# Feed-forward of a decoder block: quadrant sums of the weights made by accumulating transfers instead of VectorE

## The chip, the cores and the metric

One Trainium2 chip, one core. The time is that of the device for one launch, in microseconds (us), as the median of several runs; beside it stands one profiled execution, from which all rows come. TensorE is PE, its weight loads PEld, VectorE is DVE, ScalarE is ACT, GpSimd is POOL, SyncE is SP. Transfers are issued from the queues of SP and of POOL, and 16 DMA engines carry them.

## The reference

One layer for 512 tokens of width 2048, in float32: a sliding-window attention and a gated linear recurrence side by side, merged, projected and added to the input, and then a dense feed-forward. The change touches the feed-forward alone:

```python
x = x + gate1 * rmsnorm(y, g_post_mix[l])
h = rmsnorm(x, g_pre_ffn[l]) * (1.0 + scale2) + shift2
gu = h @ w_ffn_in[l]                       # 2048 x 11264
g_ffn, u_ffn = jnp.split(gu, 2, axis=-1)
y = (jax.nn.silu(g_ffn) * u_ffn) @ w_ffn_out[l]   # 5632 x 2048
x = x + gate2 * rmsnorm(y, g_post_ffn[l])
```

## The kernel before

Every product is made of three matmuls: each operand is split into a rounded part (`hi`, cast by ACT, line 136) and the rest (`lo`, subtracted by DVE, line 137), and TensorE adds hi*hi, hi*lo and lo*hi (lines 908 to 910). A weight chunk is 128 x 1024 float32, 512 KB. It feeds 12 matmuls of 512 columns.

Both matrices of the feed-forward are multiplied by a seven-product scheme for 2 x 2 blocks: weights and activations are cut into four quadrants, and each of the seven products takes a quadrant, or a sum or difference of quadrants, on either side. `weight_form` fetches the weight side of product i for chunk c. Products 1, 2 and 3 take a quadrant as it is; 5, 6, 7 and 4 take combinations, of which 5, 6 and 4 are built up one from the other in a buffer that is kept (`kept["t", c]`).

The up stage (`up_product`) goes through 11 groups of hidden columns, each with 7 products of 4 chunks. Its weights lie in a pool `ffs`, tag `bq`, 10 buffers; the split ones in `ffw`, tags `bhi` and `blo`, 3 buffers each. Two groups run their products 1 and 2 first, while the second half of the tokens is still being normed (`norm1`), turned and put into forms (`to_h2_second`). Products add up in pairs of PSUM banks; ACT copies them out (line 931), and DVE adds later ones (`add`, line 936). What comes out of a group is turned, combined and split into seven forms, which `put` writes to DRAM (`f_dram`, line 987, from POOL's queue, tile `fs`, 2 buffers).

The down stage runs in two parts, of 6 and of 5 groups, each part with 7 products of 12 and 10 chunks. For each pair of chunks a form is read back (`fa`, line 1105, POOL's queue, 6 buffers). Kept weights have a pool of their own (`dlt`, tag `tq`, 12), the others `dlq`, tag `bq`, 15.

PE's order is written out by hand; DVE, ACT, POOL and SP are ordered by a scheduler that follows priorities (`tc.high_priority`). Pools lie on a stack: `ffw` and `ffs` take the place of the pools of the stage before (`stage`, with `wraw`, `whi`, `wlo`; `G1`; `xr`, `G1b`, `junk` of the norm), so a first use waits for the last reader of what lay there.

Of the kernel before, what the change touches and what calls it, by code (L numbers as in the profile page):

```python
# [15 lines left out]
P = 128  # L16
# [57 lines left out]
def kernel(  # L74
# [568 lines left out]
    with tc.tile_pool(name="mrg", bufs=1, reuse_waits="tile") as mp:  # L643
# [13 lines left out]
        def late_ada(pool, i, post):  # L657
# [13 lines left out]
            else:  # L671
# [6 lines left out]
                nc.vector.tensor_tensor(out=dst, in0=dst, in1=pm, op=ALU.mult)  # L678
# [75 lines left out]
    def turn(half, c, neg=False):  # L754
        pt = bg_bank().rearrange("p (k i t) -> p k i t", k=2, i=2)
        for kk in range(2):
            k = 2 * c + kk
            for i in range(2):
                nc.tensor.transpose(pt[:, kk, i], y1[half][:, i, k * P:(k + 1) * P], ident)
        for kk in range(2):  # L760
            k = 2 * c + kk
            t, at = (nab, k - 8) if neg else (ab[:, 1], k)
            nc.scalar.activation(out=rows(half, c)[:, kk], in_=pt[:, kk], func=AF.Identity, scale=t[:, 0, at:at + 1],
                                 bias=t[:, 1, at:at + 1])
# [11 lines left out]
    fx = []  # L776

    def neg_split(hi, lo, src):
        nc.scalar.mul(hi, src, -1.0)
        nc.vector.scalar_tensor_tensor(out=lo, in0=src, scalar=-1.0, in1=hi.bitcast(F32), op0=ALU.mult, op1=ALU.subtract)  # L780

    def to_h2_second(wait):

        yield wait
        fx.extend((ffs.tile([P, 3, 2, 256], F32R, name=f"fxh{c}"), ffs.tile([P, 3, 2, 256], F32R, name=f"fxl{c}"))
                  for c in range(4))
# [4 lines left out]
        for c in range(4):  # L791
            turn(1, c + 4, True)
            split(*places(apair[c + 4], 1), rows(1, c + 4))
            yield 1
            turn(1, c)
            nc.vector.tensor_tensor(out=rows(1, c + 4), in0=rows(1, c), in1=rows(1, c + 4), op=ALU.subtract)
            split(*places(apair[c], 1), rows(1, c + 4))
            yield 1
# [69 lines left out]
    def weight_form(i, c, load, kept, keep):  # L868

        if i == 1:  # L870
            b = load(0, 0, c, "t" if keep else "b")
            if keep:
                kept["t", c] = b
            return b
        if i == 2:
            b = load(1, 0, c, "b")
            if keep:
                kept["r", c] = b
            return b
# [12 lines left out]
        if i == 7:  # L892
            b = load(0, 1, c, "b")
            sub(b, kept["q", c], b)
            return b
# [16 lines left out]
    def up_product(j, i, st, keep=True):  # L912
# [15 lines left out]
        def copy():  # L928
            t = ccp.tile([P, 2, 512], F32, name="cc", tag="cc", bufs=2) if i == 1 else fft[0].tile([P, 2, 512], F32, name="cd", tag="cd", bufs=2)
            for tb in range(2):  # L930
                nc.scalar.copy(out=t[:, tb], in_=bank[tb])
            return t

        def add(t):
            for tb in range(2):
                nc.vector.tensor_tensor(out=t[:, tb], in0=t[:, tb], in1=bank[tb], op=ALU.add)
# [3 lines left out]
        elif i == 5:  # L940
            st["c22"] = copy()
        elif i == 6:
            st["c12"] = copy()
        elif i == 3:
            add(st["c12"])
# [29 lines left out]
    def hid_forms(j, st):  # L975
# [28 lines left out]
        sub(s4, a12, s2)  # L1004
# [72 lines left out]
    for part, js in enumerate((range(0, 6), range(6, NGRP))):  # L1077
        kept, bank = {}, {}
        for i in ((1, 5, 6, 3, 7, 2, 4) if part == 0 else (2, 1, 5, 6, 3, 7, 4)):
# [156 lines left out]
```

## Time and profile before

| | |
|---|---|
| median of 3 runs | 2752.44 us (2750.15 to 2755.02) |
| the profiled execution | 2752.75 us, span 2751.0 us |
| PE busy | 2654.1 us, 96% of the span |
| DVE busy | 1983.3 us, 72% |
| ACT busy | 1238.2 us, 45% |
| POOL busy | 117.6 us |
| moved by DMA | 535.48 MB, mean 195 GB/s |

Busy shares are means over stages. The feed-forward is the part from 1386 us to 2738 us of the span; which engine a stretch waits for has to be read there. A matmul's duration (389 ns) is longer than the distance between two of them, since they overlap.

### The profile page before, as it was taken

What the parts mean: (1) busy time and instruction counts of PE and PEld (TensorE: products, weight loads), DVE (VectorE), ACT (ScalarE), POOL (GpSimd) and SP (SyncE); (2) the same over time, 40 slices, a digit from 0 to 9 for tenths busy, and PEclk for the clock granted to TensorE, in tenths of its full rate; (3) what the DMA queues carried; (4) which work ended last, traced back from release to release, by engine and by line L of the source; (5) the groups of instructions that cost most, each with busy time, mean ns of one, the idle gap of its engine ahead of it and who ended that gap; (6) DMA issues with size and microseconds to landing.
All of it is one profiled execution on the core that took longest, in us unless ns stands there. A gap on an engine that the chain in (4) does not pass through costs nothing.

```text
span 2751.0 us, 35914 instructions
## 1 busy us (share of the span) xinstructions
PE 2654.1 (96%) x13936; PEld 2154.4 (78%) x13936; DVE 1983.3 (72%) x2825; ACT 1238.2 (45%) x1735; POOL 117.6 (4%) x220
## 2 busy tenths in 40 slices
PE   6999999999999999999978999999999998999998
PEld 4777777888788888888766788888888876778886
DVE  6655549777777787455577788888778875875788
ACT  4236565565322222245564445555455553434434
POOL 0000000000000000000000000000000001100000
PEclk9999999999999999999989999999999998999999
DMA  8832222222677777456654655555555557777754
GB/s 346 318 107 79 79 81 91 83 90 77 247 257 271 263 280 263 141 184 203 223 224 155 215 173 177 178 186 179 184 184 184 183 185 293 277 259 281 246 180 162
DMA packets 132266, 535.48 MB, mean 195 GB/s; under 512 B 15424, under 2 KB 15680, under 8 KB 117376
## 3 DMA queue, kind: packets, MB, share of 16 engines
q1 hardware_dynamic: 105136, 430.48, 45.1%
q0 software_dynamic: 26816, 102.54, 10.2%
q8 instruction: 109, 1.79, 0.3%
q14 instruction: 61, 0.50, 0.1%
q10 hardware_dynamic: 144, 0.17, 0.0%
HBM read 478.08 MB, written 54.00 MB: 193 GB/s over the span
## 4 chain that ended last, share of the span: by engine, by line
PE 66%; DVE 9%; DMA 5%; issue 4%; ACT 1%; POOL 0%; DVEq 0%; ACTq 0%; POOLq 0%; SPq 0%
PE acc L909 12%; PE acc L908 12%; PE acc L910 12%; PE acc L141 9%; PE acc L143 9%; PE acc L142 9%; DVE blo L137 2%; DMA bq<-in_w_fi_dram 2%; DMA bq<-in_w_fo_dram 2%; DVE bq L866 2%; DVE wlo L130 1%; PE bg L971 1%; DVE scT L465 1%; ACT bhi L136 1%; PE bg L455 0%
## 5 line engine op out<-in xcount | busy, mean ns | idle before, releaser
L136 ACT CAST bhi<-bq 128x1024 fp32r<-128x1024 f32 x374 | 394.2, 1054 | 477.3 <-PE acc L910 428.5
L137 DVE TENSOR_TENSOR blo<-bq,bhi 128x1024 fp32r<-128x1024 f32 x374 | 456.4, 1223 | 169.9 <-ACT bhi L136 163.9
L129 ACT CAST whi<-wraw 128x1024 fp32r<-128x1024 f32 x244 | 256.3, 1051 | 565.8 <-PE acc L142 376.7
L130 DVE TENSOR_TENSOR wlo<-wraw,whi 128x1024 fp32r<-128x1024 f32 x244 | 298.1, 1223 | 184.5 <-ACT whi L129 179.9
L141 PE MATMUL acc<-ahi,whi 128*128 128x512 f32 x896 | 364.4, 407 | 1.8 <-ACT whi L129 1.8
L143 PE MATMUL acc<-ahi,wlo 128*128 128x512 f32 x896 | 351.1, 392 | 0.7 <-DVE wlo L130 0.7
L142 PE MATMUL acc<-alo,whi 128*128 128x512 f32 x896 | 351.0, 392 | 0.0
L908 PE MATMUL acc<-bhi,ahi 128*128 128x512 f32 x704 | 284.0, 403 | 32.7 <-ACT bhi L136 12.5
L909 PE MATMUL acc<-blo,ahi 128*128 128x512 f32 x704 | 278.5, 396 | 1.4 <-DVE blo L137 1.4
L910 PE MATMUL acc<-bhi,alo 128*128 128x512 f32 x704 | 278.2, 395 | 0.0
L866 DVE TENSOR_TENSOR bq<-bq 128x1024 f32<-128x1024 f32 x198 | 240.9, 1224 | 49.1 <-DMA bq<-in_w_fi_dram 34.5
L909 PE MATMUL acc<-blo,fa 128*128 128x512 f32 x616 | 241.9, 393 | 7.5 <-DVE blo L137 7.5
L254 DVE SCALAR_TENSOR_TENSOR adaacc<-ada,first,adaacc 128x512 f32<-128x512 f32 x256 | 191.7, 750 | 75.2 <-DMA ada<-in_ada_l_dram 37.6
L908 PE MATMUL acc<-bhi,fa 128*128 128x512 f32 x616 | 241.2, 392 | 4.2 <-ACT bhi L136 4.1
L910 PE MATMUL acc<-bhi,fa 128*128 128x512 f32 x616 | 240.4, 390 | 0.0
L141 PE MATMUL acc<-whi,ahi 128*128 128x512 f32 (+1 forms) x512 | 204.5, 399 | 3.6 <-ACT ahi L136 2.4
L909 PE MATMUL acc<-blo,fxh 128*128 128x512 f32 x528 | 206.0, 390 | 0.7 <-DVE blo L137 0.6
L908 PE MATMUL acc<-bhi,fxh 128*128 128x512 f32 x528 | 205.9, 390 | 0.0
L910 PE MATMUL acc<-bhi,fxl 128*128 128x512 f32 x528 | 205.5, 389 | 0.0
L143 PE MATMUL acc<-whi,alo 128*128 128x512 f32 (+1 forms) x512 | 199.3, 389 | 2.7 <-DVE alo L137 2.7
L141 PEld LDWEIGHTS acc<-ahi,whi 128*128 128x128 f32 x896 | 169.3, 189 | 41.2 <-issue 5.8
L143 PEld LDWEIGHTS acc<-ahi,wlo 128*128 128x128 f32 x896 | 169.1, 189 | 38.3 <-DVE wlo L130 1.5
(277 smaller groups left out, 4362.9 us busy)
## 6 DMA issues: line engine op xcount, KB each, us to landing
bq<-in_w_fi_dram SPq DMA_DIRECT2D x240, 512.0 KB, 3.8
ada<-in_ada_l_dram SPq DMA_DIRECT2D x64, 1024.0 KB, 6.4
bq<-in_w_fo_dram SPq DMA_DIRECT2D x98, 512.0 KB, 4.6
f_dram<-fs POOLq DMA_DIRECT2D x77, 512.0 KB, 3.3
fa<-f_dram POOLq DMA_DIRECT2D x77, 512.0 KB, 4.6
ada<-in_ada_r_dram SPq DMA_DIRECT2D x32, 1024.0 KB, 7.6
wraw<-in_w_gate_dram SPq DMA_DIRECT2D x64, 512.0 KB, 3.9
wraw<-in_w_out_dram SPq DMA_DIRECT2D x64, 512.0 KB, 3.4
```

What stands on the lines that cost most here:

```text
L129: nc.scalar.copy(out=hi[:, :width], in_=raw[:, :width])
L130: nc.vector.tensor_tensor(out=lo[:, :width], in0=raw[:, :width], in1=hi[:, :width].bitcast(F32), op=ALU.subtract)
L136: nc.scalar.copy(out=hi, in_=src)
L137: nc.vector.tensor_tensor(out=lo, in0=src, in1=hi.bitcast(F32), op=ALU.subtract)
L141: nc.tensor.matmul(pt, lhsT=ahi, rhs=bhi, start=first, stop=False)
L142: nc.tensor.matmul(pt, lhsT=ahi, rhs=blo, start=False, stop=False)
L143: nc.tensor.matmul(pt, lhsT=alo, rhs=bhi, start=False, stop=last)
L254: nc.vector.scalar_tensor_tensor(out=acc[:, :width], in0=t[:, j * width:(j + 1) * width], scalar=c_sb[:, kc:kc + 1], in1=acc[:, :width], o ...
L866: nc.vector.tensor_tensor(out=out, in0=a, in1=b, op=ALU.subtract)
L908: nc.tensor.matmul(bank[tb], lhsT=ahi[:, ts_], rhs=bhi[:, cs], start=first, stop=False, **kw)
L909: nc.tensor.matmul(bank[tb], lhsT=ahi[:, ts_], rhs=blo[:, cs], start=False, stop=False, **kw)
L910: nc.tensor.matmul(bank[tb], lhsT=alo[:, ts_], rhs=bhi[:, cs], start=False, stop=last, **kw)
```

## The change

The combinations of weight quadrants are no longer made by DVE. The kept buffer is loaded with one quadrant, split, and then a transfer from POOL's queue adds the next quadrant to it in SBUF (`join`, `accum_op=ALU.add`). A transfer can add but not subtract, so the signs of the scheme move: some activation forms, evictions and the gain of the second norm carry a minus. Product 3 now loads its quadrant afresh (it was kept from product 6), product 2 is never kept, product 4 adds its quadrant by a transfer. For each chunk position the scheme then has 4 plain loads and 4 joins in a group, where it had 5 loads and 4 subtractions on DVE (6 loads where product 2 or 4 loads afresh).

Besides: in the down stage `fa` is read from SP's queue instead of POOL's; the tag `bq` there has 12 buffers instead of 15. In the up stage the weight buffers `ffs` come first on the stack, then the activation forms, then `ffw`.

```diff
-    nab = nb.tile([P, 2, KC // 2], F32, name="nab")
-    nc.vector.tensor_scalar(out=nab, in0=ab[:, 1, :, 8:16], scalar1=-1.0, scalar2=None, op0=ALU.mult)
...
-            nc.vector.tensor_tensor(out=a12, in0=a12, in1=s2, op=ALU.subtract)
+            nc.vector.tensor_tensor(out=a12, in0=a12, in1=s2, op=ALU.add)
...
+    ffs = upx.enter_context(tc.tile_pool(name="ffs", bufs=1, reuse_waits="tile"))
+    ffx = upx.enter_context(tc.tile_pool(name="ffx", bufs=1, reuse_waits="tile"))
+    fx = [(ffx.tile([P, 3, 2, 256], F32R, name=f"fxh{c}"), ffx.tile([P, 3, 2, 256], F32R, name=f"fxl{c}")) for c in range(4)]
     ffw = upx.enter_context(tc.tile_pool(name="ffw", bufs=1, reuse_waits="tile"))
-    ffs = upx.enter_context(tc.tile_pool(name="ffs", bufs=1, reuse_waits="tile"))
...
-        if i == 5:
-            if ("t", c) not in kept:
-                kept["t", c] = load(0, 0, c, "t")
-            b = load(0, 1, c, "b")
-            sub(kept["t", c], b, kept["t", c])
-            return kept["t", c]
-        if i == 6:
-            kept["q", c] = load(1, 1, c, "b")
-            sub(kept["t", c], kept["q", c], kept["t", c])
-            return kept["t", c]
-        if i == 3:
-            return kept["q", c]
-        if i == 7:
-            b = load(0, 1, c, "b")
-            sub(b, kept["q", c], b)
-            return b
-        if ("r", c) not in kept:
-            kept["r", c] = load(1, 0, c, "b")
-        sub(kept["t", c], kept["t", c], kept["r", c])
-        return kept["t", c]
+    def weight_form(i, c, load, quad, kept, keep):
+
+        def join(t, kh, nh):
+            nc.gpsimd.dma_start(t, quad(kh, nh, c), accum_op=ALU.add)
+
+        with tc.high_priority(offset=80):
+            if i in (1, 5, 6, 4):
+                if c not in kept:
+                    kept[c] = load(0, 0, c, "t" if keep else "b")
+                t = kept[c]
+                if i != 1:
+                    join(t, *{5: (0, 1), 6: (1, 1), 4: (1, 0)}[i])
+                if not keep:
+                    del kept[c]
+                return t
+            t = load(*{2: (1, 0), 3: (1, 1), 7: (0, 1)}[i], c, "b")
+            if i == 7:
+                join(t, 1, 1)
+            return t
...
-            st["c22"] = copy()
+            st["c22"] = copy(-1.0)
...
-        put(4, a22, neg_split)
+        put(4, a22)
...
-                             "tq" if tag == "t" else "bq", 12 if tag == "t" else 15)
+                return wtile(dlt if tag == "t" else dlq, quad(kh, nh, c), "tq" if tag == "t" else "bq", 12)
...
-                        nc.gpsimd.dma_start(fas[j].bitcast(F32).rearrange("p h m t -> p (h m t)"), f_dram[i - 1, j])
-                    b = wsplit(dlw, weight_form(i, (j, cg), load, kept, i != 2 or part == 0))
+                        nc.sync.dma_start(fas[j].bitcast(F32).rearrange("p h m t -> p (h m t)"), f_dram[i - 1, j])
+                    b = wsplit(dlw, weight_form(i, (j, cg), load, quad, kept, True))
```

Three places show what the change does to the order. The first is ACT at the end of the norm, where the feed-forward begins: `junk` and `y` are rows of the norm, `rstd` its root, `CAST bhi<-bq` the split of a first weight chunk. Before:

```order
L831 ACTIVATE junk_10340,ssq<-acc 128x512
L831 ACTIVATE junk_10341,ssq<-acc 128x512
L204 ACTIVATE rstd<-rstd 128x1
L741 ACTIVATE y_1_10337,ssq<-xr_10342 128x1024 x2
L204 ACTIVATE rstd<-rstd 128x1 x2
L741 ACTIVATE y_1_10337,ssq<-xr_10343 128x1024 x2
L204 ACTIVATE rstd<-rstd 128x1
L136 CAST bhi<-bq 128x1024 x6
```

And now:

```order
L827 ACTIVATE junk_10340,ssq<-acc 128x512
L827 ACTIVATE junk_10341,ssq<-acc 128x512
L204 ACTIVATE rstd<-rstd 128x1
L744 ACTIVATE y_1_10337,ssq<-xr_10342 128x1024
L136 CAST bhi<-bq 128x1024
L744 ACTIVATE y_1_10337,ssq<-xr_10342 128x1024
L136 CAST bhi<-bq 128x1024 x2
L204 ACTIVATE rstd<-rstd 128x1 x2
L136 CAST bhi<-bq 128x1024
L744 ACTIVATE y_1_10337,ssq<-xr_10343 128x1024
L136 CAST bhi<-bq 128x1024
```

The first cast stood behind all four squares of the norm and stands behind the first of them now; the next ones stand between the others.

The second place is DVE ahead of the pair of adds `cc<-cc,acc` of the second group (line 936 before, 927 now), some 25 us later. `L866 bq<-bq` is a subtraction of weight quadrants, `fxl` and `y` belong to the forms of the activations. Before:

```order
L866 TENSOR_TENSOR bq<-bq 128x1024
L137 TENSOR_TENSOR blo<-bq,bhi 128x1024
L137 TENSOR_TENSOR fxl_11762<-y_1_10337,fxh_11761 128x512
L866 TENSOR_TENSOR bq<-bq 128x1024
L137 TENSOR_TENSOR fxl_11764<-y_1_10337,fxh_11763 128x512
L811 TENSOR_TENSOR y_1_10337<-y_0_10336,y_1_10337 128x2x2x128
L866 TENSOR_TENSOR bq<-bq 128x1024
L137 TENSOR_TENSOR fxl_11766<-y_1_10337,fxh_11765 128x512
L811 TENSOR_TENSOR y_1_10337<-y_0_10336,y_1_10337 128x2x2x128
L866 TENSOR_TENSOR bq<-bq 128x1024
L137 TENSOR_TENSOR fxl_11768<-y_1_10337,fxh_11767 128x512
L936 TENSOR_TENSOR cc<-cc,acc 128x512 x2
```

And now:

```order
L137 TENSOR_TENSOR blo<-bq,bhi 128x1024
L137 TENSOR_TENSOR fxl_11710<-y_0_10336,fxh_11709 128x512
L137 TENSOR_TENSOR fxl_11704<-y_1_10337,fxh_11703 128x512
L137 TENSOR_TENSOR blo<-bq,bhi 128x1024
L137 TENSOR_TENSOR fxl_11706<-y_1_10337,fxh_11705 128x512
L137 TENSOR_TENSOR fxl_11708<-y_1_10337,fxh_11707 128x512
L137 TENSOR_TENSOR blo<-bq,bhi 128x1024
L807 TENSOR_TENSOR y_1_10337<-y_0_10336,y_1_10337 128x2x2x128
L927 TENSOR_TENSOR cc<-cc,acc 128x512 x2
```

Between the adds of the first group and these, 6 subtractions, one `blo`, one `fxl` and one `y` have gone from DVE's queue.

The third place is POOL's queue in the up stage, where it held the writes of forms alone (a run of 70, then the reads of the down stage). Before:

```order
L987 DMA f_dram<-fs 128x1024 x70
L1105 DMA fa<-f_dram 128x1024 x8
L987 DMA f_dram<-fs 128x1024 x2
L1105 DMA fa<-f_dram 128x1024 x2
L987 DMA f_dram<-fs 128x1024
```

And now, in one group of the steady part:

```order
L869 DMA bq<-in_w_fi_dram 128x1024 x8
L978 DMA f_dram<-fs 128x1024 x2
L869 DMA bq<-in_w_fi_dram 128x1024 x4
L978 DMA f_dram<-fs 128x1024 x2
L869 DMA bq<-in_w_fi_dram 128x1024 x2
L978 DMA f_dram<-fs 128x1024 x2
L869 DMA bq<-in_w_fi_dram 128x1024 x2
L978 DMA f_dram<-fs 128x1024
```

Sixteen joins (line 869) stand in the same queue as the seven writes, and a write waits until the joins ahead of it are issued.

## Rows read from the trace of the kernel before

**Rows 1.** The page's busy line of PE and DVE.

```profile
PE 2654.1 (96%) x13936; PEld 2154.4 (78%) x13936; DVE 1983.3 (72%) x2825; ACT 1238.2 (45%) x1735; POOL 117.6 (4%) x220
```

**Rows 2.** Windows: stretch, length, busy us (count) of five engines, clock, DMA share, GB/s.

```profile
1386.00:1410.00 24.00, 10.11 (x30) 6.89 (x29) 14.99 (x24) 10.34 (x20) 1.08 (x2) 0.64 0.60 233
...
1451.00:1470.00 19.00, 8.51 (x26) 6.49 (x25) 15.09 (x19) 5.01 (x6) 0.00 (x0) 0.64 0.14 49
...
1507.00:1521.00 14.00, 10.86 (x38) 7.88 (x37) 9.82 (x12) 5.07 (x7) 1.06 (x2) 0.76 0.99 368
...
1663.00:1741.00 78.00, 78.00 (x354) 64.56 (x353) 64.06 (x64) 40.88 (x48) 3.72 (x7) 1.00 0.55 182
...
2266.00:2282.00 16.00, 9.46 (x30) 6.97 (x29) 9.28 (x9) 3.87 (x4) 0.00 (x0) 0.68 0.28 93
...
2298.00:2309.00 11.00, 6.24 (x18) 4.35 (x17) 7.22 (x7) 3.91 (x5) 0.00 (x0) 0.69 0.79 303
2309.00:2420.00 111.00, 108.98 (x483) 88.73 (x482) 85.25 (x80) 53.14 (x62) 15.35 (x29) 1.00 0.80 309
2420.00:2472.00 52.00, 48.24 (x208) 38.26 (x207) 42.09 (x40) 17.90 (x17) 4.76 (x9) 1.00 0.78 259
2472.00:2690.00 218.00, 216.80 (x955) 178.87 (x954) 156.35 (x149) 90.18 (x92) 21.12 (x40) 1.00 0.69 241
```

**Rows 3.** Waits of PE, 1386 to 2738 us: total, times, longest.

```profile
PE acc L908 <- ACT bhi L136: 16.6, 2, 12.5
PE acc L908 <- DVE cc L936: 10.5, 1, 10.5
PE acc L908 <- DVE cd L936: 9.6, 4, 4.7
PE acc L909 <- DVE blo L137: 9.4, 14, 1.7
```

**Rows 4.** Timeline where the feed-forward begins: start, length, engine; idle before in brackets.

```profile
1386.82 36.38 SPq L856 DMA_DIRECT2D bq<-in_w_fi_dram  x18
...
1389.89 1.06 ACT L741 ACTIVATE y<-xr 128x1024 f32<-128x1024 f32 x1 [2.06 <-DVE xr L740]
...
1398.45 1.03 ACT L136 CAST bhi<-bq 128x1024 fp32r<-128x1024 f32 x1
...
1399.54 0.79 PE L908 MATMUL acc<-bhi,ahi 128*128 128x512 f32 x1 [12.52 <-ACT bhi L136]
```

**Rows 5.** Timeline of DVE, 1438 to 1464 us, between the two pairs of adds.

```profile
1438.85 1.29 DVE L936 TENSOR_TENSOR cc<-cc,acc 128x512 f32<-128x512 f32 x2
...
1460.35 1.23 DVE L866 TENSOR_TENSOR bq<-bq 128x1024 f32<-128x1024 f32 x1
1462.09 1.30 DVE L936 TENSOR_TENSOR cc<-cc,acc 128x512 f32<-128x512 f32 x2
```

**Rows 6.** Groups of line 866: count, busy us, mean ns, idle before.

```profile
L866 DVE TENSOR_TENSOR bq<-bq 128x1024 f32<-128x1024 f32 x198 | 240.9, 1224 | 49.1 <-DMA bq<-in_w_fi_dram 34.5 <-DMA bq<-in_w_fo_dram 13.7
...
L866 DVE TENSOR_TENSOR tq<-bq,tq 128x1024 f32<-128x1024 f32 x44 | 53.0, 1224 | 0.1
...
L866 DVE TENSOR_TENSOR tq<-tq,bq 128x1024 f32<-128x1024 f32 x22 | 26.8, 1224 | 7.4 <-DMA bq<-in_w_fo_dram 7.1
```

**Rows 7.** Timeline of PE: twelve matmuls apart, at full clock.

```profile
2264.96 0.39 PE L910 MATMUL acc<-bhi,fxl 128*128 128x512 f32 x1
...
2267.68 0.39 PE L910 MATMUL acc<-bhi,fxl 128*128 128x512 f32 x1
```

**Rows 8.** Window at the start of the down stage; columns as in Rows 2.

```profile
2304.00:2354.00 50.00, 47.32 (x203) 37.49 (x203) 36.01 (x37) 24.71 (x32) 7.45 (x14) 0.96 1.03 415
```

**Rows 9.** DMA issues of the page: count, KB each, median us to landing.

```profile
f_dram<-fs POOLq DMA_DIRECT2D x77, 512.0 KB, 3.3
fa<-f_dram POOLq DMA_DIRECT2D x77, 512.0 KB, 4.6
```

**Rows 10.** A wait of ACT, 1386 to 2738 us.

```profile
ACT fs L136 <- DMA f_dram<-fs: 18.9, 13, 4.0
```

More of the change, by code (lines that the diff above doesn't have):

```diff
@@ L677, in late_ada @@
                     nc.gpsimd.dma_start(dst, g_post[1][:, sl])
-                nc.vector.tensor_tensor(out=dst, in0=dst, in1=pm, op=ALU.mult)
+                if i in (12, 13):
+                    nc.vector.scalar_tensor_tensor(out=dst, in0=dst, scalar=-1.0, in1=pm, op0=ALU.mult, op1=ALU.mult)
+                else:
+                    nc.vector.tensor_tensor(out=dst, in0=dst, in1=pm, op=ALU.mult)
                 if i >= 12:
@@ L761, in turn @@
             k = 2 * c + kk
-            t, at = (nab, k - 8) if neg else (ab[:, 1], k)
-            nc.scalar.activation(out=rows(half, c)[:, kk], in_=pt[:, kk], func=AF.Identity, scale=t[:, 0, at:at + 1],
-                                 bias=t[:, 1, at:at + 1])
+            nc.scalar.activation(out=rows(half, c)[:, kk], in_=pt[:, kk], func=AF.Identity, scale=ab[:, 1, 0, k:k + 1],
+                                 bias=ab[:, 1, 1, k:k + 1])
     def places(pair, half):
@@ L791, in to_h2_second @@
         for c in range(4):
-            turn(1, c + 4, True)
-            split(*places(apair[c + 4], 1), rows(1, c + 4))
+            a21, a22 = rows(1, c), rows(1, c + 4)
+            turn(1, c + 4)
+            split(*places(apair[c + 4], 1), a22)
             yield 1
             turn(1, c)
-            nc.vector.tensor_tensor(out=rows(1, c + 4), in0=rows(1, c), in1=rows(1, c + 4), op=ALU.subtract)
-            split(*places(apair[c], 1), rows(1, c + 4))
+            nc.vector.tensor_tensor(out=a22, in0=a21, in1=a22, op=ALU.subtract)
+            split(*places(apair[c], 1), a22)
             yield 1
@@ L926, in up_product, with copy, add @@
                 bg.tick()
-        def copy():
+        def copy(sign=1.0):
             t = ccp.tile([P, 2, 512], F32, name="cc", tag="cc", bufs=2) if i == 1 else fft[0].tile([P, 2, 512], F32, name="cd", tag="cd", bufs=2)
             for tb in range(2):
-                nc.scalar.copy(out=t[:, tb], in_=bank[tb])
+                if sign < 0:
+                    nc.scalar.mul(t[:, tb], bank[tb], sign)
+                else:
+                    nc.scalar.copy(out=t[:, tb], in_=bank[tb])
             return t
-        def add(t):
+        def add(t, op=ALU.add):
             for tb in range(2):
-                nc.vector.tensor_tensor(out=t[:, tb], in0=t[:, tb], in1=bank[tb], op=ALU.add)
+                nc.vector.tensor_tensor(out=t[:, tb], in0=t[:, tb], in1=bank[tb], op=op)
         if i == 1:
@@ L944, in up_product @@
         elif i == 3:
-            add(st["c12"])
+            add(st["c12"], ALU.subtract)
         elif i == 2:
@@ L1003, in hid_forms @@
         s4 = tmp()
-        sub(s4, a12, s2)
+        nc.vector.tensor_tensor(out=s4, in0=a12, in1=s2, op=ALU.add)
         put(3, s4)
@@ L1023 @@
         for i in (5, 6, 3, 7, 4) if j < 2 else (1, 5, 6, 3, 7, 2, 4) if j < NGRP - 1 else (1, 2, 5, 6, 7, 4, 3):
-            up_product(j, i, st, keep=not (i == 2 and j == NGRP - 1))
+            up_product(j, i, st)
     upx.close()
@@ L1085, with quad @@
             fas = {}
+            def quad(kh, nh, c):
+                return w_fo[((c[1] * 2 + kh) * 2 + nh) * NGRP + c[0]]
             def load(kh, nh, c, tag):
-                return wtile(dlt if tag == "t" else dlq, w_fo[((c[1] * 2 + kh) * 2 + nh) * NGRP + c[0]],
-                             "tq" if tag == "t" else "bq", 12 if tag == "t" else 15)
+                return wtile(dlt if tag == "t" else dlq, quad(kh, nh, c), "tq" if tag == "t" else "bq", 12)
             def evict(cg, tb):
                 dst, src = quarter(*where[put_to[i]], cg, tb), bank[chain][cg][tb]
-                if part == 0 and i in (1, 5, 6, 4):
+                if part == 0 and i == 5:
+                    nc.scalar.mul(dst, src, -1.0)
+                elif part == 0 and i in (1, 6, 4):
                     nc.scalar.copy(out=dst, in_=src)
                 else:
-                    nc.vector.tensor_tensor(out=dst, in0=dst, in1=src, op=ALU.add)
+                    nc.vector.tensor_tensor(out=dst, in0=dst, in1=src, op=ALU.subtract if i in (5, 3) else ALU.add)
                 if part == 1 and i == 7:
```

31 lines of the change are left out of this document (8 added, 23 removed).

## The prediction

> **What bounds the kernel now.** I read the page's busy line first: PE is busy for 96% of the span, DVE for 72% [rows 1]. So whatever DVE is spared is worth only what PE waits for it, and the windows and PE's waits say where that is [rows 2, 3]. In the steady up stage PE is busy for 78.00 of 78.00 us per group: nothing is to be had there. The lost time lies in a few places. I work it out as the window's length less its matmuls at full pace, 2.72 us for twelve [rows 7], that is 0.227 each (some records can be missing, so these are rough):
>
> - 1386 to 1410: 30 matmuls, 6.8 us of work in 24: 17.2 lost.
> - 1451 to 1470: 26, 5.9 in 19: 13.1 lost.
> - 1507 to 1521, which holds short transposes too: idle 3.1, and 10.9 busy at a clock of 0.76, some 2.6 more: 5.7 lost.
> - 2266 to 2282: 30, 6.8 in 16: 9.2 lost.
> - 2298 to 2309: 18, 4.1 in 11: 6.9 lost.
> - the down stage from 2309 to 2690: idle 2.0, 3.8 and 1.2 in three windows: 7.0 lost.
>
> Together 59 us, 2.1% of the time: the most that the change could give. PE's waits name the releasers: ACT's `bhi` once for 12.5, DVE's `cc` once for 10.5, DVE's `cd` four times for 9.6, `blo` 14 times for 9.4 [rows 3]. After each long wait the granted clock of the window is 0.64 to 0.76 [rows 2], so a wait costs more than its own length.
>
> **The change, part by part.**
>
> *Subtractions.* 264 instructions of line 866 leave DVE (198 + 44 + 22), 1.224 us each, 321 us of busy time [rows 6]. In the steady stage this is hidden already and gives nothing. Where DVE is late it counts:
>
> - First group's end. Between the two pairs of adds `cc` DVE takes 1462.1 - 1438.9 = 23.2 us [rows 5]. Of this queue go 6 subtractions and one `blo`, 1.22 us each [rows 6], and two pieces of half the width: some 9.5 us, as they overlap a little. One subtraction more is gone from the queue before. PE waits 10.5 there [rows 3], so all but about 1 us goes, and with it the slow clock: -12 of 13.1.
> - The `cd` waits of DVE, 9.6 us in four [rows 3], lie in the windows 1507 and 2266. There adds that free a PSUM pair stand behind subtractions. Without them: -5 of 5.7 and -8.5 of 9.2.
> - The `blo` waits of the down stage [rows 2, 3]: -6 of 7.0.
>
> *First buffers and order.* The first load of the feed-forward is issued at 1386.8, when PE has left the old buffers, but its cast runs at 1398.5, behind four squares of the norm; the first of them ends at about 1391 [rows 4]. Now buffers free earlier, and the cast stands behind the first square. It can start at 1391.1 instead of 1398.5: -7.3. What stays is DVE's norm between the splits. If the loads are as late as before nothing of the 7.3 comes. At 2298 PE waits for ACT, whose casts stand behind an activation that waits for the last adds; three casts now come ahead of it: -5 of 6.9.
>
> Sum of gains: 12 + 5 + 8.5 + 6 + 7.3 + 5 = 44 us.
>
> *Transfers.* The weights come in 360 transfers of 512 KB before (240 + 120) and 536 after (184 + 88 plain, 176 + 88 joins), 92 MB more. The price of a join is not in the trace. A plain transfer at full load: 0.524 MB at 415 GB/s, with the DMA share at 1.03 [rows 8], is 1.26 us of all 16 engines. From below, a join costs as much as a plain one, if reading what lies in SBUF goes beside the rest. From above three times as much: reading one operand, reading the other and writing the sum, one after the other, each as long as a plain transfer. I take two: a plain transfer reads once and writes once at the same time, a join has to read twice, and its write can go beside.
>
> The row shows 1.26 us for a plain transfer and nothing of a join [rows 8]. The Trainium skill (Collectives: The Full Stack, section "The bandwidth ceiling: the fold count and why AG ≠ RS ≠ AR") says that a reducing transfer is slow for its two source reads in one queue, not for the addition, and gives a ratio of 1.93; no run here shows it yet. By it the down stage below would pay some 10 us; by the row alone, nothing.
>
> Up stage, per group: 16 plain + 7 writes + 16 joins, so 39 transfers' worth at a price of one, 55 at two, 71 at three; times 1.26 that is 49, 69 and 90 us, against 78 us of PE [rows 2]. At two it is still hidden, with 9 us to spare. If the cover is gone, each group costs its excess, 12 us at three.
>
> Joins and writes share POOL's queue. A write waits for the joins ahead of it, and ACT's casts `fs` wait for a write to land, since `fs` has two buffers: 18.9 us in 13 waits now, 4.0 at most [rows 10], with 3.3 us to landing [rows 9]. Behind ACT stand the next casts `bhi`, and PE behind them with two chunks (5.4 us) of stock. A write behind one join lands some 2.5 us later. I take 1 us of loss for each of about 8 groups: +8 (0 to 30).
>
> A join needs the split of the product before, four chunks (10.9 us) ahead. Issue, landing (3.3 to 4.6 us for plain ones [rows 9]), 1.3 more, and the split (1.03 on ACT, 1.22 on DVE [rows 4, 6]) fit.
>
> Down stage, with 12 and 10 chunks per product. In plain transfers, product by product in part 0, reads of `fa` included (6): 18, 30, 30, 18, 42, 18, 30 at a price of two. PE's time for a product is 12 x 2.72 = 32.6 us, room for 25.8. Added up, demand is 138 against 129.2 after product 7: 8.8 short, 11.1 us. Part 1 (15, 15, 25, 25, 15, 35, 25 against 21.5 each) ends 4.3 short, 5.4 us. So +16.5, hidden by nothing: here the transfers become the bound. At one it is 0, at three 67 + 56 = +123. `fa` moves to SP's queue, in order behind loads that wait for buffers; with six buffers it is read ahead, so nothing; if it came late, 4.6 us per read [rows 9], part of the fourth case below.
>
> Signs and copies with a scale cost what the plain ones cost; product 3's fresh load is counted.
>
> Sum: -44 + 8 + 16.5 = -19.5. On the profiled execution (2752.75, its span of 2751.0 and 1.75 around it) that is 2733; it stands 0.3 above the median, so I forecast **2733 us**, 2715 to 2750 for this case alone.
>
> **The rivals.**
>
> - *A join costs as much as a plain transfer.* No DMA bound anywhere (39 x 1.26 = 49 of 78 us). For it: at 182 GB/s in the up stage engines are half idle. Against: a second operand must be read somewhere. -44 with little given back: 2709.
> - *A join costs well over two, and the down stage becomes a DMA stage.* For it: the start of the down stage shows the engines full at 415 GB/s with plain transfers alone [rows 8]. Against: the same row shows PE at 95% meanwhile. The gain of 44 - 8 is eaten where the shortfalls reach 36 us, at a price of 2.2. At 2.5 the shortfalls are 37 + 31 in the down stage and 1.5 us in each of 11 groups of the up stage: 2752.75 - 44 + 8 + 84 = 2801. This is the slower side, and it decides by one number.
> - *Order in the queues.* Writes land late behind joins, ACT stands at `fs`, and casts reach PE late. Three waits of 1 to 2 us beyond the stock in each of ten groups, +40 in place of +8: 2765. For it: ACT waits for these writes now, though POOL holds nothing else [rows 10]. Against: the stock of 5.4 us.
>
> **How the numbers follow.** Chances: the forecast 0.47, plain price 0.18, dear joins 0.23, queue order 0.12. A change within 0.2% (5.5 us) is about what a measurement here cannot tell from none. Faster: 0.18 + 0.43 of the forecast's + 0.01 = 0.62. Slower: 0.23 and 0.07 of the last: 0.30. The rest, 0.08, is the same. The range goes from 2703, a little under the plain price, to 2795, a price just under 2.5; left out are 0.03 below and 0.15 above.
>
> **What would show it.** DVE has no line 866 on weights, and its busy time falls by some 300 us. The first matmul of the feed-forward starts about 7 us sooner, and the waits of PE for `cc` and `cd` are gone. The length of the packets on POOL's queue gives the price of a join: at two they take about twice a plain packet. In the down stage the share of DMA is near 1 through product 7, and PE waits there for `bhi` or `blo` that wait for transfers. The forecast is wrong if joins are dear (shares at 1 in the up stage as well, groups longer than 78 us), if ACT's waits for `f_dram` grow to tens of us, or if the first loads come no earlier.

## The result, and the profile after

| | median us | runs | ratio to before, 95% interval |
|---|---|---|---|
| before | 2751.3 | 4 (2749.5 to 2755.0) | 1 |
| changed kernel | 2853.8 | 4 (2852.3 to 2856.3) | 1.0372 (1.0354 to 1.0390) |

Slower by 102 us, where 2733 was forecast with a range of 2703 to 2795. The page of the changed kernel, its busy line, the software queue of DMA, which carries POOL's transfers (packets, MB, share of 16 engines), and the chain that ended last:

```profile
PE 2687.8 (94%) x13936; PEld 2162.1 (76%) x13936; DVE 1695.6 (59%) x2560; ACT 1228.8 (43%) x1735; POOL 309.5 (11%) x407
...
q0 software_dynamic: 53744, 200.60, 31.0%
...
PE 50%; DMA 22%; DVE 6%; issue 4%; ACT 3%; POOL 0%; SPq 0%; ACTq 0%; POOLq 0%; DVEq 0%
```

The same chain on the page of the kernel before:

```profile
PE 66%; DVE 9%; DMA 5%; issue 4%; ACT 1%; POOL 0%; DVEq 0%; ACTq 0%; POOLq 0%; SPq 0%
```

DVE is rid of 288 us [rows 1]. In the chain the transfers' part went from 5 to 22%. Where PE lost its time stands in the windows (columns as in [rows 2]): two stretches at the start of the feed-forward, one group of the steady up stage and two parts of it, and three places of the down stage. The DMA share is the recorded time of the packets over that of 16 engines, so it can pass 1.

```profile
1386.00:1410.00 24.00, 14.79 (x52) 11.47 (x53) 17.00 (x27) 13.27 (x24) 1.08 (x2) 0.79 0.91 351
1451.00:1470.00 19.00, 18.42 (x82) 14.93 (x81) 8.11 (x7) 8.17 (x9) 4.31 (x5) 1.00 1.05 201
...
1771.00:1858.00 87.00, 81.81 (x346) 66.24 (x345) 46.84 (x47) 40.23 (x48) 17.89 (x23) 0.94 0.87 226
1801.00:1831.00 30.00, 28.09 (x116) 22.55 (x115) 16.92 (x16) 12.43 (x12) 0.86 (x1) 0.94 0.61 203
1831.00:1861.00 30.00, 29.19 (x137) 23.80 (x135) 15.80 (x17) 15.44 (x22) 10.96 (x14) 1.00 1.04 237
2380.00:2430.00 50.00, 31.17 (x113) 23.38 (x112) 16.73 (x19) 14.60 (x20) 8.18 (x11) 0.80 1.05 321
2480.00:2530.00 50.00, 37.88 (x160) 30.57 (x159) 16.11 (x15) 14.07 (x15) 10.24 (x12) 0.88 1.06 275
2654.00:2704.00 50.00, 50.00 (x222) 41.42 (x221) 29.48 (x29) 21.62 (x23) 15.60 (x18) 1.00 1.01 254
```

The first two windows are won: 52 and 82 matmuls stand where the kernel before had 30 and 26 at the same times, and the first matmul of the feed-forward starts 8.6 us sooner [rows 4]:

```profile
1390.93 0.80 PE L893 MATMUL acc<-bhi,ahi 128*128 128x512 f32 x1 [5.01 <-ACT bhi L136]
```

But a group, with the same work, now takes 87 us in place of 78, and the down stage has stretches with PE at 62 and 76%. The DMA share is the thing to read: 1.04 in one 30 us of the group and 0.61 in the other, and 1.05 in the down stage at 275 to 321 GB/s, less than the 415 of [rows 8]. A full share alone does not stop PE: from 2654 to 2704 it is 1.01, and PE is busy for 50.00 of 50. The waits of PE and ACT over the feed-forward of the changed kernel:

```profile
PE acc L893 <- ACT bhi L136: 66.7, 25, 11.7
PE acc L894 <- DVE blo L137: 38.6, 56, 2.1
...
PE acc L893 <- DVE cc L927: 1.0, 1, 1.0
...
PE acc L893 <- DVE cd L927: 0.4, 1, 0.4
```

```profile
ACT bhi L136 <- DMA bq<-in_w_fi_dram: 166.4, 70, 8.5
ACT fs L136 <- DMA f_dram<-fs: 125.0, 26, 16.2
ACT bhi L136 <- DMA bq<-in_w_fo_dram: 71.0, 20, 17.6
```

`cc` and `cd` are gone from 20.1 us to 1.4 [rows 3]; `bhi` went from 16.6 to 66.7 and `blo` from 9.4 to 38.6. ACT, the releaser of `bhi`, waits for transfers: for joined weights, and 125 us (18.9 before, [rows 10]) for the writes of `fs`. How one such wait reaches PE is in ACT's timeline near the start of a product 6, and in PE's:

```profile
1851.69 1.05 ACT L136 CAST bhi<-bq 128x1024 fp32r<-128x1024 f32 x1 [1.58 <-DMA bq<-in_w_fi_dram]
1854.18 1.06 ACT L136 CAST bhi<-bq 128x1024 fp32r<-128x1024 f32 x1 [1.44 <-DMA bq<-in_w_fi_dram]
1860.47 0.62 ACT L136 CAST fs<-sraw 128x512 fp32r<-128x512 f32 x1 [5.24 <-DMA f_dram<-fs]
1861.00 1.04 ACT L136 CAST bhi<-bq 128x1024 fp32r<-128x1024 f32 x1
```

```profile
1862.09 0.51 PE L893 MATMUL acc<-bhi,fxh 128*128 128x512 f32 x1 [1.90 <-ACT bhi L136]
1863.35 0.79 PE L894 MATMUL acc<-blo,fxh 128*128 128x512 f32 x1 [0.75 <-DVE blo L137]
```

ACT stands 5.24 us at a cast of `fs` whose buffer has not been written out; the weight's cast behind it comes late, and PE runs out of stock. The DMA issues of the steady stage (1684 to 2162 us; last number: median us to landing):

```profile
bq<-in_w_fi_dram SPq DMA_DIRECT2D x91, 512.0 KB, 4.9
bq<-in_w_fi_dram POOLq DMA_DIRECT2D x85, 512.0 KB, 9.6
f_dram<-fs POOLq DMA_DIRECT2D x38, 512.0 KB, 8.5
```

A write that landed in 3.3 us [rows 9] takes 8.5, a join 9.6, out of the 10.9 us that a product of four chunks lasts. The trace of before already held such landings, in the window of [rows 8] with its share of 1.03 (issues from 2304 to 2354, plain transfers alone):

```profile
bq<-in_w_fo_dram SPq DMA_DIRECT2D x24, 512.0 KB, 15.6
...
f_dram<-fs POOLq DMA_DIRECT2D x7, 512.0 KB, 7.4
```

### The profile page after: what moved, and what is told of

Same layout as the page of the kernel before. It is cut to its first block, busy times and chain, and to the rows that moved or that the text cites. A ratio compares the mean times of both kernels' runs of the same rounds, so it can differ in the third digit from the quotient of the medians.

```text
span 2850.5 us, 36265 instructions
## 1 busy us (share of the span) xinstructions
PE 2687.8 (94%) x13936; PEld 2162.1 (76%) x13936; DVE 1695.6 (59%) x2560; ACT 1228.8 (43%) x1735; POOL 309.5 (11%) x407
## 4 chain that ended last, share of the span: by engine, by line
PE 50%; DMA 22%; DVE 6%; issue 4%; ACT 3%; POOL 0%; SPq 0%; ACTq 0%; POOLq 0%; DVEq 0%
DMA bq<-in_w_fi_dram 10%; PE acc L141 9%; PE acc L143 9%; PE acc L142 9%; PE acc L894 7%; PE acc L895 7%; PE acc L893 7%; DMA f_dram<-fs 5%; DMA bq<-in_w_fo_dram 4%; DVE blo L137 2%; ACT bhi L136 2%; DMA tq<-in_w_fo_dram 2%; DVE scT L465 1%; DVE wlo L130 0%; PE bg L455 0%
## 5 line engine op out<-in xcount | busy, mean ns | idle before, releaser
L893 PE MATMUL acc<-bhi,fxh 128*128 128x512 f32 x528 | 214.6, 407 | 28.5 <-ACT bhi L136 27.8
L894 PE MATMUL acc<-blo,fxh 128*128 128x512 f32 x528 | 216.8, 411 | 21.2 <-DVE blo L137 21.1
L869 POOL DMA_DIRECT2D bq<-in_w_fi_dram x176 | 153.9, 917 | 591.6 <-DMA bq<-in_w_fi_dram 391.2
L895 PE MATMUL acc<-bhi,fxl 128*128 128x512 f32 x528 | 212.5, 402 | 0.0
## 6 DMA issues: line engine op xcount, KB each, us to landing
tq<-in_w_fo_dram POOLq DMA_DIRECT2D x66, 512.0 KB, 24.2
bq<-in_w_fo_dram SPq DMA_DIRECT2D x66, 512.0 KB, 15.1
```

What stands on the lines that cost most here:

```text
L869: nc.gpsimd.dma_start(t, quad(kh, nh, c), accum_op=ALU.add)
L893: nc.tensor.matmul(bank[tb], lhsT=ahi[:, ts_], rhs=bhi[:, cs], start=first, stop=False, **kw)
L894: nc.tensor.matmul(bank[tb], lhsT=ahi[:, ts_], rhs=blo[:, cs], start=False, stop=False, **kw)
L895: nc.tensor.matmul(bank[tb], lhsT=alo[:, ts_], rhs=bhi[:, cs], start=False, stop=last, **kw)
```

## The experiments

All times are medians, all ratios against the kernel before, run beside.

### Is it the price of a join, or its place in the queue?

**plain**: `nc.gpsimd.dma_start(t, quad(kh, nh, c), accum_op=ALU.add)` loses its `accum_op`, so the sums of quadrants are left out.

> The joins become plain transfers into the same tiles, same queue, same order, same waits; the sums of quadrants are left out, so products 5, 6, 7 and 4 work on wrong weights. Theory A (load): a join's packets take 328 ns against 159 ns, and most joins of a group must run in some 55 us of it, where the DMA share is now 1.03 to 1.06; at the plain price the share falls to about 0.6, groups take 78 us again, the down stage loses little: 2752 - 31 (gains kept) - 0 to 10 = 2710 to 2725. Theory B (order in POOL's queue: joins stand behind joins whose loads come late, writes behind joins): place and order are unchanged, so groups stay above 84 us, ACT's waits for f_dram stay near 125 us, and the time stays above 2800.

Measured: 2711.3 us, 0.985 (0.9832 to 0.9868). Its windows of a steady group and of the down stage, and its issues in the same stretch as above:

```profile
1678.00:1756.00 78.00, 78.00 (x354) 64.56 (x352) 46.66 (x48) 40.65 (x48) 12.22 (x23) 1.00 0.76 262
2346.00:2396.00 50.00, 50.00 (x223) 41.40 (x222) 22.15 (x19) 21.60 (x23) 8.01 (x16) 1.00 0.96 378
2480.00:2530.00 50.00, 50.00 (x222) 41.40 (x222) 23.42 (x21) 21.91 (x23) 1.20 (x3) 1.00 0.73 268
```

```profile
bq<-in_w_fi_dram POOLq DMA_DIRECT2D x96, 512.0 KB, 5.2
f_dram<-fs POOLq DMA_DIRECT2D x42, 512.0 KB, 4.4
```

Same instructions, same queues, same order: 78.00 of 78.00 again, and in these windows nothing lost in the down stage. Theory B, the order by itself, falls. The 143 us between this run and the changed kernel are what joining costs over moving the same bytes. (The run takes away two things at once, a join's longer packets and its longer issue on POOL; POOL is busy for 17.9 us of 87 in a group of the changed kernel, so the packets are the likelier, but no run parts them.) The run also gives the price. Its page has the same packets in the software queue:

```profile
q0 software_dynamic: 53744, 200.60, 20.8%
```

31.0% of 16 x 2850.5 us less 20.8% of 16 x 2707.1 us is 5130 us more for the 264 x 128 packets of the joins, 152 ns each, on a mean of 168 ns. A join's packet takes about 1.9 plain ones; by the medians of the packet records, 328 ns against 159 ns, it is 2.06.

### Which stage pays?

**up_only**, **down_only**, **sums_dve** keep the changed kernel's signs and first buffers and make the sums of one stage, the other, or both by DVE additions of separate loads, as before the change:

```diff
-            if i != 1:
-                join(t, *{5: (0, 1), 6: (1, 1), 4: (1, 0)}[i])
+        if i == 5:
+            b = load(0, 1, c, "b")
+            plus(kept["t", c], kept["t", c], b)
```

> Joins in the up stage alone; the down stage adds its quadrants on DVE, with the buffers and the queue of fa as before the change. From the losses against PE's pace in the two traces (1520 to 2295: 86.4 after, 6.8 before; start and end of the up stage 31 less than before): groups of 87 us as in the changed kernel, down stage as before: 2752 - 31 + 80 = 2801, plus or minus 8. If the up stage suffers from the down stage's transfers it is less.

> Joins in the down stage alone; the up stage adds its quadrants on DVE, the signs and the place of the first buffers are those of the changed kernel. The down stage loses 61.8 us against PE's pace after the change and 10.5 before: 2752 + 51, less what the first buffers' place gives (7 to 10): 2795, plus or minus 10. If the losses of the down stage come from a late start of its loads because of the up stage, under 2775.

> No joins at all: the changed kernel's signs and first buffers, with the sums as additions on DVE. If the earlier start of the feed-forward (first matmul at 1390.9 in place of 1399.5) comes from the place of the buffers alone: 2752 - 8 = 2744, with the wait for cc at about 1450 back. If it needs DVE free of subtractions: 2750 to 2753, no change.

Measured: up_only 2808.0 (1.0198, 1.0175 to 1.0221), down_only 2788.8 (1.0133, 1.0115 to 1.0152), sums_dve 2744.9 (0.9968, 0.9957 to 0.9978). Each within 7 us of what was expected; both stages pay, and signs and first buffers alone give 8.6 us. In sums_dve the wait for `cc` is back at 10.5 us, so the earlier first matmul does not need DVE freed of subtractions.

### How many joins does a group bear?

**half56**, **half74**, **j564**, **j567** join only the products named, in all groups of the up stage (`if i in joined: join(...)`, else `plus(...)`); the down stage adds on DVE.

> Up stage: products 5 and 6 join, 7 and 4 add on DVE; down stage adds on DVE. Work of the transfers in a group: 23 plain x 1.27 + 8 joins x 2.6 = 50 us of 78. Theory A1 (a local peak: the joins of 5 and 6 can only run between the splits of the products before them and their own, two products of 10.9 us, and the 7 writes of the hidden forms fall there as well: 8 x 2.6 + 7 x 1.27 = 30 us against 22): much of the loss stays, groups of 82 to 86 us, 2765 to 2800. Theory A2 (the whole demand, 75 to 78 us of 78 in the changed kernel, or the joins of 4 and 7 that stand among those of 5 and 6 in POOL's queue): groups of 78 to 79 us, 2725 to 2740.

> Up stage: products 7 and 4 join, 5 and 6 add on DVE; down stage adds on DVE. Transfers in a group: 27 plain x 1.27 + 8 joins x 2.6 = 55 us of 78, more than with 5 and 6 joined. Theory A1 (local peak of 5 and 6): these joins may run over three products before they are needed, so groups of 78 to 79 us and 2725 to 2745. Theory A2 (whole demand): also no loss, since 55 is less than 78; the pair of runs tells by the difference: with A1 this one is faster by 30 us or more though it moves more, with A2 the two agree within 15 us.

> Up stage: products 5, 6 and 4 join, 7 adds on DVE; down stage adds on DVE. Transfers per group: 23 plain x 1.27 + 12 joins x 2.6 = 60 us of 78. Eight joins cost 1 to 1.5 us per group (half56, half74), sixteen cost 9. Theory A2 (whole demand): what counts is how near the sum comes to the 78 us, so 60 costs 1 to 3 us per group: 2745 to 2765, and the same for 5, 6 and 7. Theory C (place in POOL's queue): these joins stand in the order in which they are needed, so 1 us per group, 2745.

> Up stage: products 5, 6 and 7 join, 4 adds on DVE; down stage adds on DVE. The same 60 us of 78 per group as with 5, 6 and 4. Two of the four joins of product 7 stand ahead of those of product 5 in POOL's queue, in the peak. Theory A2 (whole demand): 2745 to 2765, within 10 us of the run before. Theory C (place in the queue): 4 to 6 us lost per group in place of 1, 2780 to 2795.

The table takes one window, 1700 to 2130 us, of each profile. Lost is worked out from PE's matmuls there: 430 us x (1 - count / 1944), 1944 being plain's count, and per group with a group taken as 87 us.

| kernel | joins a group | median us | ratio (95%) | matmuls | lost per group | DMA share |
|---|---|---|---|---|---|---|
| sums_dve | 0 | 2744.9 | 0.9968 (0.9957 to 0.9978) | 1940 | 0.2 | 0.53 |
| half56 | 8 | 2747.7 | 0.9985 (0.9972 to 0.9998) | 1916 | 1.3 | 0.73 |
| half74 | 8 | 2760.4 | 1.0032 (1.0019 to 1.0046) | 1896 | 2.1 | 0.80 |
| j564 | 12 | 2799.0 | 1.0174 (1.0154 to 1.0194) | 1754 | 8.5 | 0.78 |
| j567 | 12 | 2805.4 | 1.0195 (1.0174 to 1.0216) | 1775 | 7.6 | 0.79 |
| up_only | 16 | 2808.0 | 1.0198 (1.0175 to 1.0221) | 1757 | 8.4 | 0.91 |
| changed kernel | 16, and in the down stage | 2853.8 | 1.0372 (1.0354 to 1.0390) | 1747 | 8.8 | 0.90 |

Theory A1 falls: half56, which keeps the joins of 5 and 6, was the faster of the pair by 13 us, not the slower by 30. The pair agrees within 15 us, as theory A2 has it, though half56 missed its 2725 to 2740. Theory A2 wants a loss that grows with the demand. Share times length of a group gives 58, 64, 68, 68 and 79 us of transfers for the five kernels with joins, from the top (groups of 79, 80, 87, 86 and 86 us); the loss jumps between 64 and 68 and then stays, though 10 us of the 78 are still free. Theory C expected 2745 for j564 and 2780 to 2795 for j567: it falls too, and so does A2's 2745 to 2765 for both. It looks like a step, not a sum; whether the transfers' time or the number of joins (8 or 12) makes it, these kernels don't tell, since both rise together. In j564 it showed as a wait at an instruction that is no join, DVE at product 7's addition, whose load lands late, with `blo` of product 3 queued behind it. SP's queue could issue that load only at 1777.0, when DVE's splits had freed a buffer, and between joins and writes it took 8.5 us to land (the median of such loads in j564 is 3.8):

```profile
1785.69 1.23 DVE L867 TENSOR_TENSOR bq<-bq 128x1024 f32<-128x1024 f32 x1 [7.55 <-DMA bq<-in_w_fi_dram]
1786.83 1.22 DVE L137 TENSOR_TENSOR blo<-bq,bhi 128x1024 fp32r<-128x1024 f32 x1
```

### Does the wait for the writes end last?

In the changed kernel: **fs3** has three buffers for `fs` (two for `sraw`), **actput** issues the writes by `nc.scalar.dma_start`; **bq8** loads the up stage's weights into 8 buffers in place of 10, **fs5bq8** has these 8 and five buffers for `fs` (two for `sraw`).

```diff
-            fs = fft[0].tile([P, 2, 2, 256], F32R, name="fs", tag="fs", bufs=2)
+            fs = fft[0].tile([P, 2, 2, 256], F32R, name="fs", tag="fs", bufs=5)
...
-            return wtile(ffs, quad(kh, nh, c), "bq", 10)
+            return wtile(ffs, quad(kh, nh, c), "bq", 8)
```

> The changed kernel with three buffers in place of two for fs (and two in place of three for sraw). Theory W (ACT waits for the landing of a write, 5.2 us at the start of product 6 in each group, and the weight's cast stands behind it): the cast of product 6 comes 4 to 5 us sooner, the 3 us stall at its start and the low clock after it (3 us more) go: 5 to 6 us in each of 9 groups, 2854 - 45 to 55 = 2800 to 2810. Theory A2 (the transfers as a whole are too slow): the stall moves to the next cast that waits for a join, less than 10 us gained, 2845 to 2854.

> The changed kernel with the writes of fs issued from ACT's queue in place of POOL's, so that they stand behind no join there. Theory W: if a write then lands in 4 to 6 us in place of 8.7, ACT's waits for f_dram fall from 125 us to under 60 and the time to 2805 to 2830; each write makes ACT wait 0.7 us for DVE besides. If the write still takes 8 us or more because the 16 engines are full of joins, the place in the queue is nothing: 2850 to 2860.

> The control: the changed kernel with eight buffers in place of ten for the weights of the up stage. The joins of product 7 then come behind those of product 4 in POOL's queue. Theory W (ACT's wait for the writes of fs ends last): the wait at the start of product 6 stays, groups of 85 to 88 us, 2840 to 2870. Theory L (loads and joins come too late for want of buffers): worse by 2 us or more per group, 2870 to 2890.

> As the control, with five buffers for fs in place of two (and two in place of three for sraw): all transfers stay, ACT no longer waits for a write of the same group. Theory W: the stall at the start of product 6 and the low clock behind it go, 5 to 6 us in each of 9 groups, 45 to 55 us less than the control. Theory A (the joins' own landing, 9 to 10 us of the 10.9 us that a product leaves, ends last): the cast then waits for the join in place of the write, less than 15 us gained.

Measured: fs3 2840.5 (1.0327, 1.0309 to 1.0345), 13 us under the changed kernel; actput 2845.1 (1.0340, 1.0321 to 1.0358), 9 under, with the writes landing in 8.1 us from ACT's queue (8.8 from POOL's in the same stretch of the changed kernel). Both times lie between the two that were expected. Neither ended the wait: ACT's `fs` still waited 36.4 and 57.0 us between 1684 and 2200 (53.7 in the changed kernel). fs5bq8 did: 2852.8 (1.0375, 1.0357 to 1.0394), against 2868.7 (1.0432, 1.0413 to 1.0451) for bq8. In 1684 to 2200 of fs5bq8, PE and ACT:

```profile
PE acc L893 <- ACT bhi L136: 33.3, 6, 6.8
PE acc L894 <- DVE blo L137: 2.8, 6, 0.5
```

```profile
ACT bhi L136 <- DMA bq<-in_w_fi_dram: 115.9, 33, 12.7
```

ACT has no wait for `f_dram` left there, and PE no longer stalls at the start of product 6: 16 us of gain. A stall is left once in each group, 5.6 us at product 7. POOL, ACT and PE there:

```profile
1786.66 0.87 POOL L869 DMA_DIRECT2D bq<-in_w_fi_dram  x1 [10.49 <-DMA bq<-in_w_fi_dram]
```

```profile
1794.48 1.04 ACT L136 CAST bhi<-bq 128x1024 fp32r<-128x1024 f32 x1 [11.55 <-DMA bq<-in_w_fi_dram]
```

```profile
1795.58 0.80 PE L893 MATMUL acc<-bhi,fxh 128*128 128x512 f32 x1 [5.58 <-ACT bhi L136]
```

A load into a buffer that came free late, then a join that cannot be issued before it lands, then the cast: 1786.66 to 1794.48 for the join alone. But the control has this stall as well, 3.4 to 5.3 us once in each group:

```profile
1804.68 0.79 PE L893 MATMUL acc<-bhi,fxh 128*128 128x512 f32 x1 [5.27 <-ACT bhi L136]
```

In the changed kernel no wait for `bhi` in that stretch is longer than 2.5 us. So the stall at product 7 comes with the eight buffers (bq8 is 15 us slower than the changed kernel), and not in place of the wait for the writes. With eight buffers theory W is right for 16 us, not for 45 to 55. What would end last with ten buffers and no wait for the writes was not run.

### Versions that beat both kernels

**ends**, **ends_dn7**, **ends_sp**, **sums_sp**, **first_sp**: joins only where PE had waited for DVE (first and last group of the up stage, or the first alone), DVE elsewhere; `_sp` reads `fa` on SP's queue as the changed kernel does, ends_dn7 besides joins product 7 of the down stage.

```diff
-                b = wsplit(ffw, weight_form(i, c, load, quad, st["kept"], keep))
+                b = wsplit(ffw, weight_mix(i, c, load, quad, st["kept"], keep and not (i == 2 and j == NGRP - 1), (5, 6, 7, 4) if j == 0 else ()))
```

> Joins only in the first and the last group of the up stage, where PE waited for DVE (cc 10.5, cd 3.4 and 7.0 us with all sums on DVE); the other groups and the down stage add on DVE. If the gain of the change comes from these places alone: 2745 less 11 (cc) less 3 (first cd) less 6 (last group) = 2725, 0.990 of before. If joins in two groups already fill the DMA engines (8 us of loss in each): 2741.

> As the run before (joins in the first and last group of the up stage), and in the down stage the sums of product 7 alone come by joins, fa on SP's queue. DVE loses 22 subtractions there, PE's blo waits of 8 us shrink: minus 3 to 6 us, 2720. If the peak theory holds for the down stage too (12 loads, 12 joins and 6 reads for one product: 18 x 1.27 + 12 x 2.6 = 54 us for 32.6 us of PE, and the products before it leave room of 32.6 - 23 = 10 each): 3 to 10 us slower, 2730.

> Joins in the first and last group of the up stage alone, all else added on DVE, reads of fa on SP's queue as in the changed kernel. The run with product 7's joins in the down stage lost 37.8 us up to 2345 where the one without (fa on POOL's queue) lost 50.6; if that is the place of fa, this run takes 2740 - 13 + 2 = 2727 to 2732; if it came from elsewhere: 2740.

> No joins, additions on DVE everywhere, reads of fa on SP's queue. With all sums on DVE and fa on POOL's queue: 2745. If fa on SP's queue gives something by itself (casts and reads at the start of the down stage earlier): 2735 to 2740; if it only helps beside joins: 2745.

> Joins in the first group of the up stage alone; all else added on DVE, fa on SP's queue. From the losses against PE's pace: 24.8 in the first group as with joins at both ends (34.3 with none), 13.0, 5.4 and 3.9 elsewhere as with no joins: 47 in place of 49.6: 2722 to 2725, no slower than with joins at both ends (2725).

| kernel | median us | ratio (95%) |
|---|---|---|
| ends | 2739.6 | 0.9951 (0.9934 to 0.9967) |
| ends_dn7 | 2746.4 | 0.9975 (0.9963 to 0.9986) |
| sums_sp | 2733.2 | 0.9928 (0.9913 to 0.9944) |
| ends_sp | 2724.8 | 0.9904 (0.9885 to 0.9923) |
| first_sp | 2723.3 | 0.9904 (0.9884 to 0.9925) |

ends missed its 2725 by 15 us, and the place of `fa` is the reason: ends_sp, with the same joins and `fa` on SP's queue, reaches it, and sums_sp, with no join at all, is 12 us faster than sums_dve. The orders of these two on DVE, ACT, SP and POOL agree up to the down stage but for those reads; in their profiled executions 9 us lie behind the last group. In sums_dve POOL's queue holds the reads of `fa` and the last writes of `fs` in one line; that the reads come late for it was not followed further. first_sp is 28 us faster than before, and the joins of the last group give nothing. Most of the 28 needs no join: signs and first buffers 9, the place of `fa` some 12, and the joins of the first group the rest, 7 to 10 (first_sp against sums_sp; their intervals overlap). Its waits of PE over the feed-forward:

```profile
PE acc L902 <- DVE cd L936: 10.5, 4, 5.5
PE acc L903 <- DVE blo L137: 5.4, 8, 1.8
PE acc L902 <- ACT bhi L136: 5.0, 1, 5.0
...
PE acc L902 <- DVE cc L936: 1.0, 1, 1.0
```

ends_dn7 against ends_sp is a small test of the down stage: the 22 joins of one product cost 21.6 us, though that stage's transfers as a whole would leave room for them. Both of its expectations, 2720 and 2730, missed that.

## Why the prediction was wrong

- **Gains, 44 us: right as a total, in part by luck.** plain keeps them all and pays for no join: 2711.3 against 2753.5 of its runs beside, 42 us. The parts shifted. First buffers 8.6 (sums_dve) for 7.3. `cc` from 10.5 to 1.0 as said. The place of `fa`, put at nothing, gave some 12 us, so the terms that were forecast at 44 gave some 30 together; whether the gains of 5 at 2298 and 6 on `blo` are partly the same microseconds, no run separates.
- **Price of a join, two: right**, 1.9 to 2.06 as above. The Trainium skill (Collectives: The Full Stack, section "The bandwidth ceiling: the fold count and why AG ≠ RS ≠ AR") gives 1.93 for reducing against copying, and the traces agree. The right price did not help: the error was in what was done with it.
- **"At two it is still hidden", +8: the step that failed first.** It cost 63 us, net of what the joins spare DVE there (up_only less sums_dve). I added 55 transfers' worth to 69 us and set them against the 78 us of a group, as if they could be spread over it. Three things in that step were off. The unit of 1.26 us was that of a full stretch; the steady stage before has 27 transfers (20 loads, 7 writes) at a share of 0.55 in 78 us [rows 2], 1.59 us each. The changed kernel's group takes 87 x 0.87 = 76 us for the 55, 1.38 each, so the 9 us to spare were not there. (That alone is not the loss: j564 loses as much with 68 us of transfers.) Joins cannot run ahead: those of 5, 6 and 4 wait for the split of the product before, those of 7 for their own load, as POOL's waits from 1684 to 2162 show, and so they bunch; a third of the group is at a share of 0.61, and the other 57 us, by the rows above, at (87 x 0.87 - 30 x 0.61) / 57 = 1.01. And in such a stretch a transfer takes not 3 to 5 us to land but 8 to 10, nearly a product's length.

```profile
POOL bq L869 <- DMA bq<-in_w_fi_dram: 241.2, 24, 34.4
...
POOL bq L869 <- DVE blo L137: 56.9, 38, 8.6
```

- **"Issue, landing (3.3 to 4.6 us for plain ones), 1.3 more, and the split fit": failed with it.** A landing of 9.6 and the split of 2.25 are 11.9 us, more than the 10.9 of a product. In half56 joins landed after 8.3 us, which makes 10.6, and the loss was 1.3 us per group; but in j564, with 8.4, it was 8.5, so this is not the whole of it. Where the prediction says that it is wrong if ACT's waits for `f_dram` grow to tens of us or groups pass 78 us, it named what came.
- **The rival of the queues, +40, chance 0.12, had one part of the mechanism**: ACT at `fs`, with the stock of 5.4 us that decides. It named the place in POOL's queue as the cause. But a write from ACT's queue lands nearly as late (8.1 us, actput), and in the same place behind plain transfers it lands after 4.4 us (plain), so it is the load of the joins on the engines. (The Trainium skill, Trainium Kernel Development and Optimization, section "Key Constraints", says that the queues of SP, ACT and POOL share the same 16 engines and that issuing from several saves only issue time; these landings, 8.1 and 8.8 us, agree.) And this wait is not the whole of it: fs5bq8, without it, gains 16 us on its control and is still 102 us slower than before.
- **Down stage, +16.5: mis-sized**, 56 us, net as well (down_only less sums_sp, which has 15 buffers for `bq` in place of 12). I let the slack of products 1, 3 and 2 carry over to 5, 6, 7 and 4. With my own numbers and nothing carried over it is, in part 0, 4.2 + 4.2 + 16.2 + 4.2 transfers, and in part 1, 3.5 + 3.5 + 13.5 + 3.5: 52.8 x 1.26 = 67 us. The measured 56 lies nearer to this than to 16.5; ends_dn7, where the slack should have covered all, says the same. What keeps it from carrying over (twelve buffers, the joins' order behind their loads) was not tried singly.
- **The slower rival** put dear joins at 2801 from a price above 2.2. The side was right, and so was the down stage as a DMA stage, but not the reason: the price was about two.

The stages pay separately: 2733 (sums_sp) + 63 + 56 = 2852, against 2854 measured.

What stays open: how the 63 us of the up stage divide between the wait for writes (some 13 to 16 by fs3 and fs5bq8), late loads (seen in j564) and late joins (seen with eight buffers), and what makes the step between 8 and 12 joins.

## What to carry to other kernels

Work that is moved onto a resource with room "on average" must be laid out in time: write down for each transfer the earliest moment at which it may start and the latest at which it is needed, and sum the load within these windows, not over the loop. Read landing times in a stretch where the share is already near 1 (here 7.4 us for a write, in the trace of before), not in the quiet one (3.3 us), and compare them with the stock that hides them. And if an engine limits only at a few places, relieve it at these places: joins in the first group alone took some 7 to 10 us off, where joins everywhere made the kernel 102 us slower.

## What the runs showed of the hardware

- An accumulating transfer into SBUF cost about 1.9 plain ones of its size on the DMA engines here (152 ns more on 168 per 4 KB packet), and its issue occupied POOL for 917 ns in the mean, against 530 ns for the plain one in the same place (changed kernel, then plain):

```profile
L869 POOL DMA_DIRECT2D bq<-in_w_fi_dram x176 | 153.9, 917 | 591.6 <-DMA bq<-in_w_fi_dram 391.2 <-DVE blo L137 146.2 <-issue 42.8
```

```profile
L869 POOL DMA_DIRECT2D bq<-in_w_fi_dram x176 | 93.3, 530 | 587.1 <-DMA bq<-in_w_fi_dram 345.5 <-DVE blo L137 219.3 <-issue 15.2
```

- With full engines both queues landed late: in the down stage of the changed kernel (share 1.05 and 1.06 in the windows above) plain loads on SP's queue landed after 15.1 us and joins after 24.2, where those of plain took 5.8 and 7.6:

```profile
tq<-in_w_fo_dram POOLq DMA_DIRECT2D x66, 512.0 KB, 24.2
bq<-in_w_fo_dram SPq DMA_DIRECT2D x66, 512.0 KB, 15.1
```

- Where PE stalled for 2.5 us near the start of a product 6 (1771.4 to 1773.9), the window from 1771 to 1781 has a granted clock of 0.67, which is a part of its time at the lower of the two levels (1.2 and 2.4 GHz):

```profile
1771.00:1781.00 10.00, 6.72 (x17) 4.86 (x16) 4.15 (x5) 5.09 (x8) 2.91 (x4) 0.67 0.96 230
```
